# Where an adaLN gate vector is computed, and in which order a Strassen-like stage splits its operands

## The chip, the cores and the metric

One core of one Trainium2 chip runs the whole program. The metric is the device time of one execution in microseconds, as the median of several executions; lower is better.

## The reference, cut to what matters

Two streams, a prompt of 1024 tokens and a sample of 64, go through two layers with the same weights. Each layer has a mixing part (layer 0: attention and a linear recurrence side by side; layer 1: a gated recurrence) and a SwiGLU feed-forward part. Both are conditioned on a vector `c` per stream:

```
sc = silu(c)
m = (sc @ w_ada[l] + b_ada[l]).reshape(B, 6, 1024)
sh1, sc1, g1, sh2, sc2, g2 = m
hn = rms_norm(x, norm_mix[l]) * (1 + sc1) + sh1
x = x + (1 + g1) * mix(hn)
hn = rms_norm(x, norm_ffn[l]) * (1 + sc2) + sh2
x = x + (1 + g2) * ((silu(hn @ wg[l]) * (hn @ wu[l])) @ wd[l])
```

The model width is 1024 (8 tiles of 128 rows, `KD`), the hidden width of the feed-forward part 2816 (22 blocks of 128, `FF`). The gate `g2` of layer 0, group 5 of `m`, is what the change moves: 1024 values for each of the two streams.

## The kernel before, in words

Everything is held transposed: features on the 128 partitions, the 1088 tokens of both streams in the free dimension. fp32 matrices are split into a high part (rounded to fp32r, a cast on ScalarE) and a low part (source minus high, on GpSimd or VectorE), and each product is done as three matmuls: high by high, low by high, high by low.

Instructions are put in order for each engine ahead of the run by a list scheduler that simulates the program. A block under `soon()` (line 76) is preferred by it, a block under `later()` (line 79) is put off. The engine names with an `o` (`oV`, `oS`, `oPE`, lines 43 to 61) keep their instructions in the order in which the program writes them, on each engine among themselves; plain `V`, `S` and `PE` leave the order to the scheduler.

**Attention stage of layer 0** (lines 624 to 1167). The loop over four steps of two heads (lines 1126 to 1155) interleaves the score products and their sigmoids (`attn_w`, lines 877 to 880), the transposes and value products (`attn_o`) and the steps of the recurrence (`hgrn`). The input projections of the steps to come are put off, as filler; each takes its weights through `load_in` (line 1080), which uses a raw tile of two buffers (`raw_tile`, line 102). `load_in` also carries the conditioning: first two tiles of 128 rows of groups 2 to 4 a call, as dot products on VectorE (`mods_dve`), then, when these are done, one tile of group 5 a call: a load of 512 KB of `ada5`, 8 matmuls of two columns into a PSUM bank (line 1096), and a copy (line 1097).

**Feed-forward stage.** `enter` and `first_block` compute block 0 of the hidden layer the plain way. `up_half` (line 425) does block 1 the plain way (`plain_block`, in four chunks of tokens) and blocks 2 to 21 with a Strassen-like scheme: **seven products** of half size instead of eight, on sums of quarters of the input and sums of quarters of the weights. `sums` (line 467) makes the input's side: it adds the shift to the 8 tiles of `x` on ScalarE, forms four differences for each of four pairs of tiles (k and k + 4), and splits three of them into T3, T1 and T4 and then the last into T2. The products use their operands in the order B11, T2, T3, T1, B21, T4, B22 (line 488). T2 lies in tiles that block 1 has been reading. `weights` (line 450) makes the weights' side for each block: the first of its seven operands is a plain quarter, the second and third need the three additions of lines 455 to 457, all in program order on VectorE. Seven weights in high and low parts go through five buffers each. The accumulators X, Y, Z and W are read between the products by short instructions (`n1` to `p3`, lines 534 to 565).

**Conditioning in the feed-forward stage** (`Ada`, line 399). `open` loads the two conditioning vectors, spread over the partitions, and takes SiLU of them as sigmoid and multiply (`load_cbc`, line 183). Then each block has the slots `n1`, `n5` and, where the block number is under 8, `n2`. A slot does one tile: it takes a raw tile that was loaded ahead into one of two buffers and forms two dot products. In `n1` both are multiply-and-sum instructions on VectorE; in `n5` and `n2` (shared) the second is a multiply on GpSimd and a sum on ScalarE (lines 193 and 194). Their by-product goes to one scratch tile, `T[6]`. After eight tiles `finish_mods` adds the bias. In layer 0's stage 40 tiles (layer 1's groups 0 to 4) are done so, in layer 1's stage 8 (group 5). The second SiLU of a block (line 551) marks `n2`.

Of the kernel before, what the change touches and what calls it, by code (L numbers as in the profile page):

```python
# [54 lines left out]
def hybrid_encoder(ctx: ExitStack, tc: tile.TileContext, I, O):  # L55
# [114 lines left out]
    def finish_mods(l, i, j0=0, j1=KD):  # L170
        m = mods[l][:, i * KD + j0:i * KD + j1, :]
        b = vec[:, V_BADA + l * 48 + i * KD + j0:V_BADA + l * 48 + i * KD + j1]
        V.tensor_add(m, m, b.unsqueeze(2).to_broadcast([P, j1 - j0, 2]))
        if i in (2, 5):
            V.tensor_scalar_add(m, m, 1.0)
        if i in (1, 4):
            w = i // 3
            g = vec[:, V_NORM + (2 * l + w) * KD + j0:V_NORM + (2 * l + w) * KD + j1]
            V.scalar_tensor_tensor(scale[l][w][:, j0:j1, :], m, 1.0, g.unsqueeze(2).to_broadcast([P, j1 - j0, 2]),
                                   ALU.add, ALU.mult)  # L180


    def load_cbc(ts, sg):
        for v in range(2):
            dma(ts[v], I["cT2"][v:v + 1, :].partition_broadcast(P))
            S.activation(sg, ts[v], AF.Sigmoid)
            V.tensor_mul(ts[v], ts[v], sg)
        return ts

    def mods_dve(l, t, cb, raw, junk, shared=False, V=V):  # L190
        for v in range(2):
            if v and shared:
                G.tensor_mul(raw, raw, cb[v])
                S.activation(junk(), raw, AF.Identity, accum_out=mods[l][:, t, v:v + 1])  # L194
            else:
                V.scalar_tensor_tensor(junk(), raw, 1.0, cb[v], ALU.mult, ALU.mult,
                                       accum_out=mods[l][:, t, v:v + 1])
# [201 lines left out]
    class Ada:  # L399


        def __init__(self, todo):
            self.todo = [(i, j) for i in todo for j in range(KD)]

        def open(self, pool, raw, junk):
            self.raw, self.junk = raw, junk
            self.cb = load_cbc([pool.tile([P, 1024], F32, name="cbc", tag="cbc", bufs=2) for v in range(2)],
                               raw())
            self.ready = []

        def fetch(self, n):
            for _ in range(min(n, len(self.todo))):
                i, j = self.todo.pop(0)
                raw = self.raw()
                dma(raw, I["adaT"][48 + i * KD + j])
                self.ready.append((i, j, raw))

        def one(self, shared):
            if self.ready:
                i, j, raw = self.ready.pop(0)  # L420
                mods_dve(1, i * KD + j, self.cb, raw, self.junk, shared, oV)
                if j == KD - 1:
                    finish_mods(1, i)

    def up_half(l, plain, x, t_tag, op_tag, ada):
        B = B12, B11, B21, B22 = plain[0]
        with phase_pool(f"up{l}") as fp:
# [38 lines left out]

            def sums():

                for k in range(KD):
                    for r0, rn, b in rng(0, NT):  # L470
                        v = x[k][:, r0:r0 + rn]
                        oS.activation(v, v, AF.Identity, bias=mods[l][:, 3 * KD + k, b:b + 1])
                T1, T3, T4 = ([halves(fp.tile([P, NT], F32R, name="op", tag=t, bufs=4)) for _ in range(4)]
                              for t in ("t1", "t3", "t4"))
                for k in range(4):
                    a, b, c, d = x[k][:, :HT], x[k][:, HT:], x[k + 4][:, :HT], x[k + 4][:, HT:]
                    V.tensor_sub(d, b, d)
                    V.tensor_sub(b, b, a)
                    V.tensor_sub(a, a, d)
                    V.tensor_sub(c, c, a)  # L480
                    split(d, T3[k][:, 0, :], T3[k][:, 1, :], V, S=oS)
                    split(b, T1[k][:, 0, :], T1[k][:, 1, :], V, S=oS)
                    split(c, T4[k][:, 0, :], T4[k][:, 1, :], V, S=oS)
                T2 = []
                for k in range(4):
                    T2.append(halves(u(op_tag, F32R, "op")))
                    split(x[k][:, :HT], T2[k][:, 0, :], T2[k][:, 1, :], V)
                return B11, T2, T3, T1, B21, T4, B22

            stage["open"].close()  # L490
            with psum_pool(f"acc{l}", *(("acc" + n, 1024, 1) for n in "XYZW")):
# [31 lines left out]
                for f in range(2, FF):  # L523
                    if f == FF - 3:
                        assert not ada.todo and not ada.ready
                        got = [hid_units(i, t_tag) for i in range(GROUPS[0])]
                    X, Y, Z, W = (new_acc(n) for n in "XYZW")
                    x_, y_, z_, w_ = (t[:, :, :Q] for t in (X, Y, Z, W))
                    i = 2 * (f % 3) if f < FF - 3 else 4 + 2 * (f % 2)
                    tg, hid = T[i], T[i + 1]  # L530
                    pair = lambda t: t.rearrange("p (j t) -> p j t", j=2)
                    t, g, hA, hB = (pair(v) for v in (tg[:, :HT], tg[:, HT:], hid[:, :HT], hid[:, HT:]))

                    def n1():
                        S.copy(t, x_)
                        ada.one(False)
                        ada.fetch(1)

                    def n6():
                        oV.tensor_sub(t, y_, t)  # L540

                    def p7():
                        oV.tensor_add(hB, z_, t)

                    def n5():
                        oV.tensor_add(hB, w_, hB)
                        ada.one(True)
                        ada.fetch(1)

                    def n2():  # L550
                        S.activation(g, x_, AF.Silu)
                        if f < 8:
                            ada.one(True)
                            ada.fetch(1)

                    def p4():
                        oV.tensor_add(hA, z_, t)
                        oV.tensor_mul(hA, hA, g)
                        dma(hid_dram[f][:, :HT], hid[:, :HT])

                    def p3():
                        oV.tensor_add(t, w_, t)
                        S.activation(t, t, AF.Silu, scale=-1.0)
                        oV.tensor_mul(hB, hB, t)
                        dma(hid_dram[f][:, HT:], hid[:, HT:])

                    for acc, op, start, use in zip((X, Y, Z, W, X, Z, W), ops, (1, 1, 1, 1, 0, 0, 0),
                                                   (n1, n6, p7, n5, n2, p4, p3)):
                        w = ahead.pop(0)
                        for j in range(2):  # L570
                            product(acc, w, op, j, start)
                        for w in itertools.islice(queue, 1):
                            ahead.append(w)
                        with soon():
                            use()
# [48 lines left out]
    with phase_pool("mix") as mp:  # L624
# [450 lines left out]
                yield  # L1075

        todo = [(i, j) for i in (2, 3, 4) for j in range(KD)]
        todo_pe = list(range(KD))

        def load_in(t):  # L1080
            w = load_w(wi[t])
            with later():
                for _ in range(min(2, len(todo))):
                    i, j = todo.pop(0)
                    raw = raw_tile()
                    dma(raw, I["adaT"][i * KD + j])
                    mods_dve(0, i * KD + j, cb, raw, lambda: mp.tile([P, 1024], BF16, name="junk", tag="junk"))
                    if j == KD - 1:
                        finish_mods(0, i)
                if not todo and todo_pe:  # L1090
                    j = todo_pe.pop(0)
                    raw = raw_tile()
                    dma(raw, I["ada5"][j])
                    ps = bank("o")
                    for e in range(KD):
                        PE.matmul(ps[:, :2], raw[:, e * P:(e + 1) * P], sc[:, e, :], start=(e == 0), stop=(e == KD - 1))
                    V.tensor_copy(mods[0][:, 5 * KD + j, :], ps[:, :2])
                    if j == KD - 1:
                        finish_mods(0, 5)
            return w  # L1100

        def out_group(g, after=None, chunks=CH):
# [88 lines left out]


    stage["open"] = banks_open
    got = up_half(0, plain, x, "B", "A", Ada(range(5)))

    xg_open = ExitStack()
    xg = xg_open.enter_context(phase_pool("xg"))
# [199 lines left out]


    xg_open.close()
    got = up_half(1, plain, x, "A", "B", Ada((5,)))  # L1400
    with phase_pool("ffn1") as fp:
        stage["w"] = fp
        layout(fp, ("hid", 2 * NT, 2), ("late", 2 * NT, 1), ("wd_lo", 1024, 6), ("w_raw", 1024, 2),
# [123 lines left out]
def _layout(i):  # L1527
# [9 lines left out]
    d["cT2"] = t(c)  # L1537
    blk = lambda w: t(w.reshape(KD, P, -1, P).transpose(2, 1, 0, 3).reshape(-1, P, KD * P))
    d["ada0"] = blk(g["w_ada"][0][:, 1024:2048])
    d["ada5"] = blk(g["w_ada"][0][:, 5120:6144])  # L1540
    aT = np.concatenate([g["w_ada"][0], g["w_ada"][1]], axis=1)
    d["adaT"] = t(aT.T.reshape(96, P, 1024))
    d["w_in_even"] = blk(g["w_in_even"][0])
# [55 lines left out]
```

## Time and profile before

| | |
|---|---|
| median of 3 runs | 2803.64 us (2800.59 to 2804.72) |
| the profiled execution, its own time | 2801.73 us |
| its span, first to last instruction | 2800.0 us |
| TensorE matmul busy | 2616.5 us (93%) |
| VectorE busy | 1855.6 us (66%) |
| GpSimd busy | 1180.6 us (42%) |
| ScalarE busy | 1022.0 us (36%) |
| mean granted TensorE clock | 0.963 |

In the rows PE is TensorE's matmuls, PEld its weight loads, DVE VectorE, ACT ScalarE, POOL GpSimd and SP the queue that issues most loads. PEclk is the granted share of full clock: 1.00 is 2.4 GHz, 0.50 is 1.2 GHz. An instruction's record can overlap the one after it, so busy times are unions. Line 51 stands for every instruction that is kept in program order. A matmul of fp32 operands leaves two records.

### The profile page before, as it was taken

How to read it: one execution, taken by the hardware profiler on the slowest of the kernel's cores; microseconds unless marked ns; L12 is line 12 of the kernel's file. 1: busy time of each engine (PE TensorE's matmuls, PEld its weight loads, DVE VectorE, ACT ScalarE, POOL GpSimd, SP SyncE). 2: the span in 40 equal slices, each digit the busy share in tenths (PEclk: the TensorE clock that was granted, in tenths of full speed). 3: DMA queues.
4: the chain of work that ended last, by engine and by line, in shares of the span. 5: the costliest groups of instructions: out<-in, count | busy, mean ns of one | idle time of the engine just before them, and what ended most of it. 6: DMA issues, size and time to landing. Idle time of an engine off the chain costs nothing. (4 is left out here: it accounts for less than half of the span.)

```text
span 2800.0 us, 44597 instructions
## 1 busy us (share of the span) xinstructions
PE 2616.5 (93%) x17680; PEld 2553.8 (91%) x17680; DVE 1855.6 (66%) x2850; ACT 1022.0 (36%) x1862; POOL 1180.6 (42%) x795
## 2 busy tenths in 40 slices
PE   5898999999988899999999979998889999999998
PEld 5898989998878899999999979988889999999997
DVE  8768763667897778876465575658877444446556
ACT  3225343354454533333221146564363222222112
POOL 6446443455441477765322233444126444433112
PEclk8999989899999999999999989999999999999999
DMA  6232111113112344443432101121223222226211
GB/s 240 91 113 92 46 58 55 57 53 130 57 50 103 108 141 133 130 138 108 152 130 94 62 16 59 68 74 63 98 74 122 70 81 83 70 92 219 89 61 64
DMA packets 99663, 261.98 MB, mean 94 GB/s; under 512 B 16640, under 2 KB 36096, under 8 KB 99456
## 3 DMA queue, kind: packets, MB, share of 16 engines
q1 hardware_dynamic: 99168, 258.03, 27.7%
q8 instruction: 139, 2.28, 0.3%
q10 hardware_dynamic: 288, 1.11, 0.1%
q14 instruction: 68, 0.56, 0.1%
HBM read 208.41 MB, written 50.69 MB: 93 GB/s over the span
## 5 line engine op out<-in xcount | busy, mean ns | idle before, releaser
L100 POOL TENSOR_TENSOR w_lo<-w_raw,w_hi 128x1024 fp32r<-128x1024 f32 x92 | 237.3, 2586 | 533.9 <-ACT w_hi L99 484.6
L100 POOL TENSOR_TENSOR wl<-wg,wh 128x512 fp32r<-128x512 f32 x164 | 225.4, 1381 | 375.6 <-ACT wh L99 333.6
L507 PE MATMUL accZ<-op,wh 128*128 128x272 f32 x1280 | 245.5, 289 | 5.8 <-DVE tmp L51 5.7
L507 PE MATMUL accW<-op,wh 128*128 128x272 f32 x1280 | 244.3, 288 | 0.0
L507 PE MATMUL accX<-op,wh 128*128 128x272 f32 x1280 | 243.5, 288 | 0.0
L99 ACT CAST w_hi<-w_raw 128x1024 fp32r<-128x1024 f32 x90 | 93.2, 1050 | 362.3 <-PE ps_mm L313 253.5
L129 PE MATMUL ps_mm<-h_hi,w_hi 128*128 128x384 f32 (+1 forms) x624 | 213.2, 342 | 2.8 <-ACT w_hi L99 1.3
L129 PE MATMUL ps_mm<-h_hi,w_lo 128*128 128x384 f32 (+1 forms) x624 | 212.4, 342 | 2.0 <-POOL w_lo L100 2.0
L129 PE MATMUL ps_mm<-h_lo,w_hi 128*128 128x384 f32 (+1 forms) x624 | 212.0, 340 | 0.0
L507 PEld LDWEIGHTS accZ<-op,wh 128*128 128x128 f32 x1280 | 201.1, 188 | 7.6 <-DVE tmp L51 6.2
L99 ACT CAST wh<-wg 128x512 fp32r<-128x512 f32 x160 | 97.5, 619 | 296.9 <-DVE wg L51 191.4
L318 DVE SCALAR_TENSOR_TENSOR x<-ps_mm,mods,x 128x384 f32<-128x384 f32 (+4 forms) x334 | 152.2, 480 | 75.1 <-PE ps_mm L313 73.9
L507 PEld LDWEIGHTS accW<-op,wh 128*128 128x128 f32 x1280 | 201.3, 188 | 0.0
L507 PEld LDWEIGHTS accX<-op,wh 128*128 128x128 f32 x1280 | 200.9, 188 | 0.0
L507 PE MATMUL accZ<-op,wl 128*128 128x272 f32 x640 | 184.6, 288 | 1.0 <-POOL wl L100 1.0
L507 PE MATMUL accX<-op,wl 128*128 128x272 f32 x640 | 184.5, 288 | 0.0
L507 PE MATMUL accW<-op,wl 128*128 128x272 f32 x640 | 184.5, 288 | 0.0
L318 DVE SCALAR_TENSOR_TENSOR x<-ps_t,mods,x 128x384 f32<-128x384 f32 (+3 forms) x220 | 107.1, 504 | 87.9 <-PE ps_t L313 87.9
L51 DVE SCALAR_TENSOR_TENSOR tmp<-hid,cbc 128x1024 f32<-128x1024 f32 x68 | 132.0, 1941 | 21.6 <-ACT tmp L194 20.9
L100 POOL TENSOR_TENSOR wl<-wu,wh 128x512 fp32r<-128x512 f32 x84 | 131.7, 1569 | 27.9 <-ACT wh L99 27.3
L507 PE MATMUL accY<-op,wh 128*128 128x272 f32 x640 | 124.7, 292 | 16.1 <-ACT wh L99 16.1
L318 DVE SCALAR_TENSOR_TENSOR x<-ps_z,mods,x 128x384 f32<-128x384 f32 (+2 forms) x198 | 91.3, 485 | 61.4 <-PE ps_z L313 60.6
(485 smaller groups left out, 8066.1 us busy)
## 6 DMA issues: line engine op xcount, KB each, us to landing
hid<-in_adaT SPq DMA_DIRECT2D x48, 512.0 KB, 3.9
w_raw<-in_wd SPq DMA_DIRECT2D x44, 512.0 KB, 3.8
hid_dram<-tmp SPq DMA_DIRECT2D x80, 272.0 KB, 2.1
hid_lo<-hid_dram SPq DMA_DIRECT2D x40, 544.0 KB, 4.7
wg<-in_wg SPq DMA_DIRECT2D x42, 512.0 KB, 3.9
wu<-in_wu SPq DMA_DIRECT2D x42, 512.0 KB, 3.6
w_raw<-in_w_in_even SPq DMA_DIRECT2D x28, 512.0 KB, 3.7
w_raw<-in_adaT SPq DMA_DIRECT2D x24, 512.0 KB, 3.6
```

The costliest lines, as they stand in the source:

```text
L51: return lambda *a, **k: self.tc.keep_in_program_order(f(*a, **k))
L99: S.copy(hi, src)
L100: (lo_eng or G).tensor_sub(lo, src, hi.bitcast(F32))
L129: PE.matmul(ps[:, :n], a[:, k * P:(k + 1) * P], b[:, c0:c0 + n], start=(i == 0), stop=(i == last))
L318: V.scalar_tensor_tensor(x[m][:, r0:r0 + rn], ps[:, r0 - c0:r0 - c0 + rn], gate[:, m, b:b + 1], x[m][:, r0:r0 + rn], ALU.mult, ALU.add)
L507: PE.matmul(acc[:, j, :Q], a[:, k * P:(k + 1) * P], op[k][:, b, c], start=(start == 1 and i == 0), stop=(i == 11), skip_group_check=True)
```

## The change

Four edits. The gate of layer 0 (group 5) leaves `load_in` and becomes the first eight tiles of the `Ada` of layer 0's seven-product stage, which so has 48. The number of blocks with a third slot is now worked out from the number of tiles: below block `thrice`, which is 16 with 48 tiles and 2 with the 8 tiles of layer 1's stage. The SiLU of the conditioning vectors is one ScalarE instruction in place. In `sums` the shift goes over the tiles in pairs, the differences come first, then the splits for T2, T3, T1 and T4 in this order, and all of it is kept in program order on VectorE and ScalarE.

```
-    def load_cbc(ts, sg):
+    def load_cbc(ts):
         for v in range(2):
             dma(ts[v], I["cT2"][v:v + 1, :].partition_broadcast(P))
-            S.activation(sg, ts[v], AF.Sigmoid)
-            V.tensor_mul(ts[v], ts[v], sg)
+            S.activation(ts[v], ts[v], AF.Silu)
...
-            self.todo = [(i, j) for i in todo for j in range(KD)]
+            self.todo = [(l, i, j) for l, i in todo for j in range(KD)]
+            self.thrice = 2 + max(0, len(self.todo) - 2 * (FF - 5))
...
-                dma(raw, I["adaT"][48 + i * KD + j])
+                dma(raw, I["adaT"][48 * l + i * KD + j])
...
-                for k in range(KD):
+                for k in (0, 4, 1, 5, 2, 6, 3, 7):
                     for r0, rn, b in rng(0, NT):
                         v = x[k][:, r0:r0 + rn]
                         oS.activation(v, v, AF.Identity, bias=mods[l][:, 3 * KD + k, b:b + 1])
...
+                T2 = []
+                part = lambda k: (x[k][:, :HT], x[k][:, HT:], x[k + 4][:, :HT], x[k + 4][:, HT:])
                 for k in range(4):
-                    a, b, c, d = x[k][:, :HT], x[k][:, HT:], x[k + 4][:, :HT], x[k + 4][:, HT:]
-                    V.tensor_sub(d, b, d)
-                    V.tensor_sub(b, b, a)
-                    V.tensor_sub(a, a, d)
-                    V.tensor_sub(c, c, a)
-                    split(d, T3[k][:, 0, :], T3[k][:, 1, :], V, S=oS)
-                    split(b, T1[k][:, 0, :], T1[k][:, 1, :], V, S=oS)
-                    split(c, T4[k][:, 0, :], T4[k][:, 1, :], V, S=oS)
-                T2 = []
+                    a, b, c, d = part(k)
+                    oV.tensor_sub(d, b, d)
+                    oV.tensor_sub(b, b, a)
+                    oV.tensor_sub(a, a, d)
                 for k in range(4):
                     T2.append(halves(u(op_tag, F32R, "op")))
-                    split(x[k][:, :HT], T2[k][:, 0, :], T2[k][:, 1, :], V)
+                    split(part(k)[0], T2[k][:, 0, :], T2[k][:, 1, :], oV, S=oS)
+                for k in range(4):
+                    split(part(k)[3], T3[k][:, 0, :], T3[k][:, 1, :], oV, S=oS)
+                for k in range(4):
+                    split(part(k)[1], T1[k][:, 0, :], T1[k][:, 1, :], oV, S=oS)
+                for k in range(4):
+                    a, b, c, d = part(k)
+                    oV.tensor_sub(c, c, a)
+                    split(c, T4[k][:, 0, :], T4[k][:, 1, :], oV, S=oS)
...
-                        if f < 8:
+                        if f < ada.thrice:
                             ada.one(True)
                             ada.fetch(1)
...
-                if not todo and todo_pe:
-                    j = todo_pe.pop(0)
-                    raw = raw_tile()
-                    dma(raw, I["ada5"][j])
-                    ps = bank("o")
-                    for e in range(KD):
-                        PE.matmul(ps[:, :2], raw[:, e * P:(e + 1) * P], sc[:, e, :], start=(e == 0), stop=(e == KD - 1))
-                    V.tensor_copy(mods[0][:, 5 * KD + j, :], ps[:, :2])
-                    if j == KD - 1:
-                        finish_mods(0, 5)
...
-    got = up_half(0, plain, x, "B", "A", Ada(range(5)))
+    got = up_half(0, plain, x, "B", "A", Ada([(0, 5)] + [(1, i) for i in range(5)]))
...
-    got = up_half(1, plain, x, "A", "B", Ada((5,)))
+    got = up_half(1, plain, x, "A", "B", Ada([(1, 5)]))
```

## Rows read from the trace of the kernel before

**Rows 1.** Busy time by stretch: stretch, length, PE, PEld, DVE, ACT, POOL, PEclk, DMA share, GB/s

```profile
340.00:560.00 220.00, 211.01 (x1322) 201.18 (x1321) 122.59 (x191) 81.99 (x187) 90.52 (x72) 0.88 0.18 56
...
750.00:800.00 50.00, 42.85 (x266) 37.07 (x265) 49.96 (x84) 32.08 (x77) 33.34 (x32) 1.00 0.21 60
946.00:1372.00 426.00, 419.37 (x3316) 417.36 (x3316) 315.02 (x336) 138.23 (x242) 276.05 (x162) 1.00 0.38 121
```

**Rows 2.** Waits of ScalarE, 340 to 560 us: us in total, times, longest

```profile
ACT om L879 <- PE ps_z L877: 22.9, 17, 3.9
```

**Rows 3.** Line 1096: its busy time, then timeline rows (start, length) of TensorE

```profile
340.00:560.00 220.00, 20.03 (x128) 21.04 (x128) 0.88 0.18 56
...
434.71 2.96 PE L1096 MATMUL ps_o<-sc,w_raw 128*128 128x2 f32 x26
437.53 1.18 PE L912 MATMUL ps_o<-wt,vs 128*128 128x256 f32 x8
...
395.63 3.51 PE L1096 MATMUL ps_o<-sc,w_raw 128*128 128x2 f32 x16
```

**Rows 4.** Busy time by stretch, short stretches of the attention stage

```profile
488.00:492.00 4.00, 4.00 (x34) 3.89 (x33) 3.72 (x8) 0.48 (x1) 3.78 (x4) 0.91 0.39 137
492.00:508.00 16.00, 15.62 (x61) 14.45 (x62) 9.00 (x12) 5.66 (x10) 7.54 (x5) 0.50 0.39 125
...
395.00:409.00 14.00, 14.00 (x59) 13.44 (x59) 9.25 (x11) 7.42 (x17) 9.33 (x7) 0.50 0.31 97
```

**Rows 5.** Timeline of ScalarE, line 551: blocks 4 to 10, then layer 1's 4 and 5

```profile
1001.11 0.62 ACT L551 ACTIVATE tmp<-accX 128x544 f32<-128x544 f32 x1 [1.05 <-PE accX L507]
...
1024.86 0.62 ACT L551 ACTIVATE tmp<-accX 128x544 f32<-128x544 f32 x1 [1.18 <-PE accX L507]
...
1046.28 0.62 ACT L551 ACTIVATE tmp<-accX 128x544 f32<-128x544 f32 x1
...
1069.34 0.62 ACT L551 ACTIVATE tmp<-accX 128x544 f32<-128x544 f32 x1
...
1091.99 0.61 ACT L551 ACTIVATE tmp<-accX 128x544 f32<-128x544 f32 x1
...
1113.74 0.63 ACT L551 ACTIVATE tmp<-accX 128x544 f32<-128x544 f32 x1 [2.37 <-PE accX L507]
...
1134.79 0.62 ACT L551 ACTIVATE tmp<-accX 128x544 f32<-128x544 f32 x1 [4.12 <-PE accX L507]
...
2148.02 0.62 ACT L551 ACTIVATE tmp<-accX 128x544 f32<-128x544 f32 x1 [1.10 <-PE accX L507]
...
2170.86 0.62 ACT L551 ACTIVATE tmp<-accX 128x544 f32<-128x544 f32 x1 [4.66 <-PE accX L507]
```

**Rows 6.** Timeline of VectorE and GpSimd in layer 0's seven-product stage

```profile
957.96 2.78 POOL L193 TENSOR_TENSOR hid<-hid,cbc 128x1024 f32<-128x1024 f32 x1 [1.90 <-DVE tmp L51]
...
958.57 2.72 DVE L51 TENSOR_TENSOR wu<-wg,wu 128x512 f32<-128x512 f32 x1
...
1006.99 0.18 DVE L173 TENSOR_TENSOR mods<-mods,vec 128x16 f32<-128x16 f32 x1 [3.74 <-ACT tmp L194]
...
1033.34 2.11 DVE L51 SCALAR_TENSOR_TENSOR tmp<-hid,cbc 128x1024 f32<-128x1024 f32 x1 [2.26 <-ACT tmp L194]
```

**Rows 7.** Timeline, start of layer 0's stage, and TensorE's longest wait there

```profile
910.30 8.83 ACT L51 ACTIVATE x<-x,mods 128x1024 f32<-128x1024 f32 x13
...
916.83 0.72 DVE L477 TENSOR_TENSOR x<-x 128x544 f32<-128x544 f32 x1 [9.09 <-ACT x L51]
...
926.68 1.22 DVE L187 TENSOR_TENSOR cbc<-cbc,hid 128x1024 f32<-128x1024 f32 x1
...
929.09 2.62 DVE L100 TENSOR_TENSOR op<-x,op 128x544 fp32r<-128x544 f32 x4
...
943.28 0.68 DVE L51 TENSOR_TENSOR wg<-s,wg 128x512 f32<-128x512 f32 x1
...
PE accY L507 <- ACT wh L99: 7.9, 1, 7.9
```

More of the change, by code (lines that the diff above doesn't have):

```diff
@@ L402, in __init__ @@
         def __init__(self, todo):
-            self.todo = [(i, j) for i in todo for j in range(KD)]
+            self.todo = [(l, i, j) for l, i in todo for j in range(KD)]
+            self.thrice = 2 + max(0, len(self.todo) - 2 * (FF - 5))
         def open(self, pool, raw, junk):
             self.raw, self.junk = raw, junk
-            self.cb = load_cbc([pool.tile([P, 1024], F32, name="cbc", tag="cbc", bufs=2) for v in range(2)],
-                               raw())
+            self.cb = load_cbc([pool.tile([P, 1024], F32, name="cbc", tag="cbc", bufs=2) for v in range(2)])
             self.ready = []
@@ L412, in fetch @@
             for _ in range(min(n, len(self.todo))):
-                i, j = self.todo.pop(0)
+                l, i, j = self.todo.pop(0)
                 raw = self.raw()
-                dma(raw, I["adaT"][48 + i * KD + j])
-                self.ready.append((i, j, raw))
+                dma(raw, I["adaT"][48 * l + i * KD + j])
+                self.ready.append((l, i, j, raw))
         def one(self, shared):
             if self.ready:
-                i, j, raw = self.ready.pop(0)
-                mods_dve(1, i * KD + j, self.cb, raw, self.junk, shared, oV)
+                l, i, j, raw = self.ready.pop(0)
+                mods_dve(l, i * KD + j, self.cb, raw, self.junk, shared, oV)
                 if j == KD - 1:
-                    finish_mods(1, i)
+                    finish_mods(l, i)
     def up_half(l, plain, x, t_tag, op_tag, ada):
@@ L1077, in hybrid_encoder @@
         todo = [(i, j) for i in (2, 3, 4) for j in range(KD)]
-        todo_pe = list(range(KD))
         def load_in(t):
@@ L1539, in _layout @@
     d["ada0"] = blk(g["w_ada"][0][:, 1024:2048])
-    d["ada5"] = blk(g["w_ada"][0][:, 5120:6144])
     aT = np.concatenate([g["w_ada"][0], g["w_ada"][1]], axis=1)
```

## The prediction

> **What bounds the kernel now.** I read the page first: TensorE is busy for 93% of the span and every other engine for two thirds or less, so a change counts where it takes TensorE work away or makes TensorE wait. The view of busy time by stretch shows this for the three places that the change touches [rows 1]. In the attention stretch from 340 to 560 us TensorE is busy 211.0 of 220 us and VectorE 122.6. At 750 to 800 VectorE is the full one, with 49.96 of 50. In the first seven-product stage, 946 to 1372, TensorE is busy 419.4 of 426, VectorE 315, GpSimd 276. The waits of ScalarE in the attention stretch then say who is late there: the sigmoids of the scores waited 22.9 us in 17 places for a score product on TensorE [rows 2]. The attention chain itself stands behind TensorE's queue, so TensorE time taken out of this stretch should come off the end.
>
> **Part 1: 64 products per condition pair leave attention.** The eight tiles of the gate are 8 x 8 matmuls of two columns. The trace has 128 records for them (two for each), busy 20.03 us [rows 3]. Their busy time overlaps the next group: the run of 26 at 434.71 lasts to 437.67, while the next matmul starts at 437.53, 0.14 us before. Some fifteen such groups make about 2 us of overlap, so I take **-18 us**. Bounds: all 128 at the pace of the run at full clock (26 in 2.96 us) 14.6 us, all at the pace of the slow run (16 in 3.51 us) 28.1 us; nothing at all if the stretch is not bound by TensorE (a rival). With them go eight 512 KB loads on SP's queue, eight small copies on VectorE, and the use of the two-buffer raw tile and of a PSUM bank between weight loads; none of these engines is full in the stretch [rows 1], so I price them at nothing, and a gain from earlier weights lies within the upper bound.
>
> **Part 2: the same tiles come back as dot products.** In the first seven-product stage 48 tiles instead of 40 are conditioned. Two per block of the hidden layer as before; a third one, so far in blocks 2 to 7, now in blocks 2 to 15. Each third is a VectorE multiply-and-sum, a GpSimd multiply of 2.78 us and a ScalarE sum, and a load. DMA engines are busy 38% there [rows 1] and take the load for nothing. The rest is not free. The start of the second SiLU marks each block [rows 5]: from block 9 to 10, with two per block, it recurs after 21.05 us, which is TensorE's own pace. From block 5 on, with three, after 21.42, 23.06 and 22.65, a mean excess of 1.33 us, with 0.70 left over in block 8. The mechanism is in rows 6: at 1033.34 the third's VectorE instruction waited 2.26 us for the ScalarE sum of the tile before it (both write the same scratch tile), and behind it in VectorE's order stand the additions that free the accumulators which TensorE needs next. Eight more such blocks cost 8 x 1.33 = 10.6 us. When a group of eight ends on a shared tile, the closing addition waits for ScalarE too (3.74 us at 1006.99), and block 4, where that happened, took 23.75, an excess of 2.70; the second half's only stretched block, 22.84, is the same case. Groups now end so in blocks 9 and 12: 2 x 1.4 more. Sum **+13.4 us**, bounds 8 x 0.37 = 3 and 8 x 2.70 = 21.6. The end values are single blocks; a mean of three is nearer to what eight will do. The gate's own values are first read after this stage, so nobody waits for them.
>
> One row also prices the shared multiply from the other side: beside the GpSimd multiply that began at 957.96 a VectorE addition took 2.72 us, while 0.72 or less is usual for this size [rows 6, 7]. The Trainium skill, SBUF — State Buffer, section Who interferes with whom, speaks against this part of the change: VectorE with two SBUF inputs and a reading GpSimd take one shared port in turns, and the loser waits for the whole instruction. The trace agrees with it (2.72 for the addition). By that alone each further multiply would put some 2.0 us on VectorE, an estimate of 16.2 us for eight in place of 13.4.
>
> **Part 3: the second half.** Its eight tiles are now spread two per block. The stretched block of 22.84 us [rows 5] should fall to the pace: **-1.8 us** (0 to -1.8).
>
> **Part 4: the start of both seven-product stages.** Today TensorE waits 7.9 us before the second product [rows 7]; the record names the cast of the weights, which stands behind a sum on VectorE that starts at 943.28, itself in a stretch of VectorE without a gap from 916.83. The change makes four edits there. (a) ScalarE shifts tiles 0, 4, 1, 5 ... in that order. Thirteen pieces take 8.83 us, so about 1.3 us for a tile; the first pair is complete after two tiles and not five, and VectorE starts 3.9 us earlier. But then pairs come each 2.6 us and three subtractions need 1.9, so the last pair's end lies at about 923.2. (b) The two 1.22 us multiplies of the conditioning vector go (Silu at once), about 2.3 us of VectorE. (c) The halves are cut in the order in which products use them: T2 no longer comes last. (d) All of it stands in program order, and so **ahead of the weight sums**, which today are put between. After 923.2 come sixteen cuts and four subtractions at 0.65 us [rows 7], 13.1 us, four multiplies of the plain block's hidden rows, some 1.6 us, and in the last group each cut must wait for the cast of what was subtracted just before it, about 0.65 us four times, half of it covered by those multiplies: 939.3 to 940.6. Then three weight sums of 0.6 to 0.7: 941.2 to 942.6, against 943.9 today. I take **-1.7 us for each stage, -3.4** together. Bounds: 0, and -7.9 each if T2 alone had been late. Silu also spares table changes on ScalarE, which is not what is late there.
>
> **Sum.** -18 + 13.4 - 1.8 - 3.4 = **-9.8 us**. The profiled execution took 2801.73 us (span 2800.0 and 1.7 around it), so 2791.9 for its like; the median of the runs is 1.9 above it, so the forecast is **2793.8 us**. A measurement of this kernel tells about 0.2%, 5.6 us, from no change: faster means under 2798.0, slower over 2809.2.
>
> **Rivals.**
> *The clock comes back too.* At 395 to 409 and at 492 to 508 the granted clock was 0.50, the 1.2 GHz level, and before the second of these TensorE was busy 4.00 of 4 us, mostly with the two-column products [rows 4]. Of these 30 us let a third be the products themselves; the other 20 us would take half at 2.4 GHz, 10 us less: 2783.8. Against it: bursts of other narrow products stand close by and may hold the clock down without these. The Trainium skill, TensorE: Matmul & The Clock Gate, Part 1, ties the lower level to idleness; by that rule removing busy matmuls gives no clock back, and the row with 4.00 of 4 does not agree with it. Chance 0.25.
> *The freed time is not on the path.* Slower: at 750 to 800 VectorE is full [rows 1], and if attention ends when VectorE's chain there ends, whatever TensorE did before, part 1 is worth nothing and the rest makes +13.4 - 5.2 = +8.2: 2811.8. It decides if VectorE's work up to there does not move ahead with TensorE's. Against it: rows 2, and VectorE's idle 97 us in the stretch. Chance 0.12.
> *The thirds pile up.* If blocks 8 to 15 each lose 2.70 us, the sum is -18 + 21.6 - 5.2 = -1.6: 2802.0, no difference that can be told. Chance 0.15.
> *T2 was the gate.* If the order of the cuts does what its form suggests, each start gives 7.9 us: -22.2, 2781.4. Against it is the late weight sum. Chance 0.08.
>
> **How the numbers follow.** The forecast case has 0.40. Its own range, with part 1 from 15 to 21 us and the thirds from 10 to 16, is 2788 to 2800. Faster takes most of it (0.36) with the clock's 0.25 and T2's 0.08, together 0.69; the same takes 0.04 and the pile-up's 0.15, 0.19; slower the uncovered path, 0.12. The range reaches from 2775, where the clock comes back and the dot products are cheaper than 1.33, to 2808, leaving the slower rival mostly out.
>
> **What would show it.** Part 1 right: no two-column products between 340 and 560, the seven-product stage starts some 18 us earlier (its first plain matmul is at about 909 today). Part 2: SiLU spacing of 22 to 23 us in blocks 4 to 15 and not only to 8. Part 3: no stretched block in the second half. Part 4: a wait before the second product of about 6 us, still for a weight. The forecast is wrong if the stage's start moves by under 10 us, if blocks 8 to 15 keep 21.05, or if attention's granted clock rises well above 0.88.

## The result, and the profile after

The changed kernel takes **2771.4 us** (median of 4 runs, 2768.4 to 2778.4) where the kernel before takes 2802.8: a ratio of 0.9897, with a 95% interval of 0.9875 to 0.9919. Run again beside other kernels it gave 0.9913 (0.9898 to 0.9928). The forecast of 2793.8 had the sign right and a third of the size, and its range began at 2775.

To see where the time went I cut the span at two marks that every version has: the first matmul of block 1's plain product in each feed-forward stage, and the second SiLU of block 21, the last. The stretches of the profiled execution, before and after, in us: up to the first mark 908.9 and 863.6 (**-45.3**); from there to block 21's SiLU 459.4 and 474.8 (**+15.4**); on to the second stage's mark 687.6 and 689.3 (+1.7); the second stage to its block 21 452.1 and 447.0 (**-5.1**); the rest 292.0 and 293.2 (+1.2). The sum is -32.1, the difference of the spans, 2800.0 and 2767.9.

**Attention.** Busy time of the changed kernel in the attention stage's middle (stretch, length, PE, PEld, DVE, ACT, POOL, PEclk, DMA share, GB/s), and the same view of the kernel before:

```profile
280.00:600.00 320.00, 310.67 (x2090) 296.47 (x2089) 214.90 (x309) 142.96 (x332) 159.37 (x129) 0.99 0.16 47
```

```profile
280.00:600.00 320.00, 309.14 (x1958) 295.18 (x1956) 188.69 (x283) 121.41 (x277) 134.36 (x109) 0.91 0.17 54
```

TensorE is as busy as it was, 97% of the stretch, so the busy column shows nothing. The clock does: 0.91 against 0.99. At two levels of 1.00 and 0.50, a mean of 0.91 over 320 us is 57.6 us at half speed, and 0.99 is 6.4 (0.98, or 12.8, in the second profile of the same kernel). In the same 320 us VectorE did 215 us of work and not 189. This is what answers to the first row of [rows 1] and to [rows 4].

**The start of the seven products.** TensorE's wait for a weight between 850 and 960 us (total, times, longest) and VectorE's timeline there, answering to [rows 7]:

```profile
PE accY L511 <- ACT wh L99: 1.9, 1, 1.9
```

```profile
889.27 0.68 DVE L51 TENSOR_TENSOR s<-wu 128x512 f32<-128x512 f32 x1
...
891.93 0.69 DVE L51 TENSOR_TENSOR wg<-s,wg 128x512 f32<-128x512 f32 x1
...
903.62 0.72 DVE L51 TENSOR_TENSOR op<-x,op 128x544 fp32r<-128x544 f32 x1 [0.71 <-ACT op L51]
```

The wait before the second product fell from 7.9 to 1.9 us. The weight sums (s at 889.27, wg at 891.93) stand ahead of the last split of T4 (903.62), not behind it.

**The thirds.** The second SiLU of blocks 8 to 13, answering to [rows 5]; a block's time is counted from its own SiLU to the next block's:

```profile
1043.47 0.61 ACT L555 ACTIVATE tmp<-accX 128x544 f32<-128x544 f32 x1
...
1066.14 0.61 ACT L555 ACTIVATE tmp<-accX 128x544 f32<-128x544 f32 x1
...
1094.71 0.63 ACT L555 ACTIVATE tmp<-accX 128x544 f32<-128x544 f32 x1 [3.25 <-PE accX L511]
...
1136.81 0.63 ACT L555 ACTIVATE tmp<-accX 128x544 f32<-128x544 f32 x1
...
1162.04 0.63 ACT L555 ACTIVATE tmp<-accX 128x544 f32<-128x544 f32 x1 [1.38 <-PE accX L511]
```

With three tiles block 8 takes 22.67 us (1043.47 to 1066.14), as such a block did before. Block 9, whose third tile ends a group, takes 28.57; blocks 10 and 11 are at TensorE's pace, 42.10 for both; block 12, where a group ends on a shared tile too, takes 25.23. What happens in block 9, on VectorE, on TensorE (in brackets the wait), and in the view by stretch:

```profile
1082.64 0.18 DVE L173 TENSOR_TENSOR mods<-mods,vec 128x16 f32<-128x16 f32 x1 [4.65 <-ACT tmp L193]
```

```profile
1083.81 0.56 PE L511 MATMUL accZ<-op,wh 128*128 128x272 f32 x2 [5.00 <-DVE tmp L51]
```

```profile
1085.00:1090.00 5.00, 5.00 (x33) 5.00 (x32) 4.24 (x8) 0.66 (x1) 0.00 (x0) 0.75 0.73 246
```

VectorE stands 4.65 us for ScalarE's sum, TensorE 5.00 behind it, and then the clock is granted at 0.75 of full over the next 5 us: 33 matmuls where the 5 us windows around it at 1.00 hold 41 to 43.

### The profile page after: what moved, and what is told of

Read it like the earlier page. It is cut to its first block, busy times and chain, and to the rows that moved or that the text cites. A ratio compares the mean times of both kernels' runs of the same rounds, so it can differ in the third digit from the quotient of the medians.

```text
span 2767.9 us, 44376 instructions
## 1 busy us (share of the span) xinstructions
PE 2588.9 (94%) x17552; PEld 2525.6 (91%) x17552; DVE 1883.2 (68%) x2856; ACT 1016.1 (37%) x1868; POOL 1204.6 (44%) x802
## 4 chain that ended last, share of the span: by engine, by line
PE 41%; DVE 8%; ACT 3%; issue 1%; DMA 0%; POOL 0%; DVEq 0%; SPq 0%; ACTq 0%; POOLq 0%
PE ps_t L312 7%; PE ps_mm L312 7%; PE ps_z L312 7%; PE accZ L511 5%; PE accW L511 5%; PE accX L511 5%; PE accY L511 2%; DVE xc L51 2%; DVE mu L51 1%; DVE rg L51 1%; PE ps_t L51 1%; ACT rg L51 1%; PE ps_z L51 1%; DVE x L317 1%; ACT mu L51 1%
## 5 line engine op out<-in xcount | busy, mean ns | idle before, releaser
L511 PE MATMUL accZ<-op,wh 128*128 128x272 f32 x1280 | 249.2, 292 | 18.8 <-DVE tmp L51 18.8
L51 DVE SCALAR_TENSOR_TENSOR tmp<-hid,cbc 128x1024 f32<-128x1024 f32 x77 | 150.9, 1960 | 36.0 <-ACT tmp L193 35.3
```

The source lines that it names most:

```text
L51: return lambda *a, **k: self.tc.keep_in_program_order(f(*a, **k))
L511: PE.matmul(acc[:, j, :Q], a[:, k * P:(k + 1) * P], op[k][:, b, c], start=(start == 1 and i == 0), stop=(i == 11), skip_group_check=True)
```

## The experiments

The theory: attention's gain is the two-column products' own time and, as much again, the clock that they cost; the thirds cost what VectorE waits for on the shared path over GpSimd and ScalarE. Rivals: the loads and the raw tile's turns held attention back; the stage start carries the gain; the thirds cost VectorE's own work. The kernel before moved between chips by up to 9 us in its median, so ratios are to the kernel before on the same chip, and the terms are read from the stretches:

| kernel | ratio to before, 95% | first mark | SiLU of block 2 after it | of block 21 | second stage, block 21 |
|---|---|---|---|---|---|
| before | 1 | 908.9 | 50.1 | 459.4 | 452.1 |
| after | 0.9897 (0.9875 to 0.9919) | 863.6 | 43.0 | 474.8 | 447.0 |
| after_again | 0.9913 (0.9898 to 0.9928) | 866.5 | 45.9 | 474.5 | 446.6 |
| e1_move_only | 0.9935 (0.9920 to 0.9950) | 870.3 | 50.0 | 478.0 | 450.5 |
| e2_start_only | 0.9968 (0.9951 to 0.9985) | 903.9 | 45.9 | 455.8 | 448.6 |
| e3_narrow | 1.0017 (1.0008 to 1.0026) | 909.1 | 43.4 | 471.9 | 446.2 |
| e4_wide | 0.9967 (0.9953 to 0.9981) | 886.8 | 43.4 | 472.0 | 444.4 |
| e5_forty | 0.9839 (0.9818 to 0.9860) | 872.5 | 43.0 | 456.0 | 445.3 |
| e6_scratch | 0.9863 (0.9842 to 0.9884) | 871.5 | 43.0 | 464.5 | 444.4 |
| e7_late | 0.9887 (0.9864 to 0.9910) | 867.4 | 46.0 | 469.8 | 443.9 |
| e8_both | 0.9883 (0.9860 to 0.9905) | 872.1 | 45.9 | 464.0 | 446.9 |
| e9_t2last | 0.9922 (0.9903 to 0.9942) | 869.7 | 46.3 | 473.2 | 448.6 |
| e10_sigmoid | 0.9925 (0.9906 to 0.9944) | 870.3 | 46.2 | 475.0 | 448.4 |
| e11_order | 0.9908 (0.9886 to 0.9930) | 864.7 | 45.8 | 474.9 | 446.2 |
| e12_load | 0.9924 (0.9900 to 0.9948) | 867.3 | 44.5 | 473.8 | 446.0 |
| e13_own_end | 0.9853 (0.9838 to 0.9867) | 868.4 | 45.8 | 457.2 | 446.6 |
| e14_thirds_dve | **0.9809** (0.9793 to 0.9826) | 869.8 | 45.8 | 445.9 | 443.7 |

**Taking the change apart: e1_move_only and e2_start_only.** The first is the changed kernel with `sums` and `load_cbc` of the kernel before; the second is the kernel before with those of the changed one.

> The changed kernel with the old start of the seven-product stages (old order of shifts, differences and splits, sigmoid and multiply for the conditioning vectors). Stage by stage the changed trace reads: attention -45 us, start of each seven-product stage -7, blocks of the first +22.5, blocks of the second -1. If these are separate effects, this kernel is 13 to 15 us slower than the changed one, about 2785, the wait before the second product is back at 8 us in both stages, and the attention stage ends as early as in the changed one. If the attention gain hangs on the new start (one common list of instructions, scheduled together), the first plain matmul of block 1 is later than 870 us.

> The kernel before with the new start of the two seven-product stages alone; the gate's conditioning stays in attention. Separate effects: about 2803 - 14 = 2789 us, first plain matmul of block 1 at 909 us as before, waits before the second product near 2 us, blocks of the first stage as before (excess of 7.4 us over blocks 2 to 8). If the weight sums stood strictly behind all splits, as the prediction had it, the wait would be about 6 us and the gain under 4 us.

The effects are separate. Where the products have left attention the first mark lies between 863.6 and 872.5 in twelve profiles (mean 868.9); with them in, at 908.9, 903.9 and 909.1 (mean 907.3): **-38 us**, and the 863.6 of the first profile was a low one. The new start alone is worth 459.4 - 455.8 = 3.6 and 452.1 - 448.6 = 3.5 us, about **-7** for both and not the 14 that I read at block 2: TensorE's wait of e1 is back at 8.0 and of e2 down at 1.9, but in the first stage the blocks with three tiles are not ready sooner and take a part back (in e2 block 2 is 4.2 us earlier, block 21 3.6), and in the second stage the clock can still fall after the short wait: 45.9 us to block 2 in eight versions whose start there is written alike, 43.4 in five others.

**The products' time or their clock: e3_narrow, e4_wide, e12_load.** The first puts line 1096's loads and products back beside the change. The others alter that block:

```
-                    for e in range(KD):
-                        PE.matmul(ps[:, :2], raw[:, e * P:(e + 1) * P], sc[:, e, :], start=(e == 0), stop=(e == KD - 1))
+                    for e in range(2 * KD):
+                        PE.matmul(ps[:, :272], w[0][:, (e % KD) * P:(e % KD + 1) * P], h[0][e % KD][:, :272],
+                                  start=(e == 0), stop=(e == 2 * KD - 1))
```

for e4_wide, and no matmul at all, the load alone, for e12_load (the load stays in e4_wide too).

> The changed kernel, with the two-column products of the gate done in attention as well (their results are copied to a spare tile that nobody reads). If it is these products and what hangs on them that cost the 45 us, the attention stage is back at about 909 us for the first plain matmul of block 1, the whole near 2771 + 45 = 2816 us, and the granted clock between 350 and 550 us falls from 1.00 to below 0.9. If only their own TensorE time counted, 18 to 20 us: about 2790.

> As the kernel with the narrow products in attention, but in their place 16 matmuls of 272 columns on operands that are there anyway (the projection's weights and input, result not read) for each of the eight tiles, 128 in all at about 0.125 us, 16 us of TensorE; the eight 512 KB loads into the same raw tile stay. If the clock is the larger part of the loss, it stays at 1.00 here and the stage ends 16 to 20 us later than in the changed kernel, about 2789 us. If the loads and the raw tile's turn-taking are the cause, it is as slow as the narrow one, about 2812 to 2816.

> The changed kernel with the eight 512 KB loads in attention as before, read by a small copy only, without any matmul. If the loads and their turn in the raw tile hold back the projections' weights, part of the 45 us returns (10 us or more); if they were free, as the prediction had it, the attention stage ends within 3 us of the changed kernel's.

The first mark comes at 909.1, 886.8 and 867.3. The loads cost nothing that the mark shows. Against the mean of 868.9, 128 wide matmuls of 0.125 us, 16 us of TensorE, cost 18; 128 records of narrow ones, busy 20.03 us [rows 3], cost 40. Each mark is that of one execution, and the one profiled of e3_narrow was the slowest of its ten (2810.6 us, median 2806.3): by the medians of the two on one chip, narrow costs 16.1 us more than wide, not 22.3. The view by stretch of e3_narrow, e4_wide and e12_load:

```profile
280.00:600.00 320.00, 310.40 (x1967) 296.25 (x1966) 189.77 (x281) 121.24 (x276) 135.19 (x110) 0.91 0.18 55
```

```profile
280.00:600.00 320.00, 309.27 (x2059) 294.48 (x2059) 209.85 (x305) 133.96 (x305) 148.78 (x121) 0.97 0.18 58
```

```profile
280.00:600.00 320.00, 312.10 (x2070) 298.62 (x2070) 214.30 (x315) 141.52 (x328) 155.28 (x129) 0.97 0.20 62
```

As many matmul records come from the same point of the program. With 272 columns the clock is 0.97, as it is with no products at all in e12_load; with 2 columns it is 0.91. So about half of attention's gain is the clock for everybody else. Which property of the narrow products takes the clock is not shown: the wide ones differ in their operands as well (fp32r instead of fp32, weights that are used anyway). The whole of e3_narrow is 10 us under the 2816 that I expected: I had added 45 us where 38 is the usual size.

**The price of the thirds: e5_forty.** `Ada([(0, 5)] + [(1, i) for i in range(4)])`.

> The changed kernel with 40 tiles of conditioning in the first seven-product stage instead of 48: the last group, layer 1's feed-forward scale, is left out and set to constants, so its conditioning is missing from the output. Thirds stop after block 7 again. If the eight thirds cost what the block spacing says, this stage is 19 to 23 us shorter and the whole about 2750 us; by the prediction's price it would be 13 us, 2758.

The first stage is 474.8 - 456.0 = **18.8 us** shorter (18.5 against the second profile), just under the first expectation's 19 and well over the 13.4 of the prediction. The whole, 2757.4 us, is near the 2758 of the second expectation, but it was measured on another chip: by the ratios to the kernel before (0.9839 against 0.9897 and 0.9913) the eight tiles cost 16 to 21 us.

**What the thirds wait for: e6_scratch, e7_late, e8_both.** A second scratch tile `T[7]` for `mods_dve`'s ScalarE sum; `finish_mods` called two slots later; both.

> The changed kernel with a second scratch tile: the by-product of the ScalarE sum goes to T[7], that of VectorE's stays in T[6]. If the thirds cost their 22 us because VectorE's next multiply-and-sum waits for ScalarE to write the same scratch tile (25 waits, 35 us on VectorE in the changed trace), the blocks with three tiles come down to 21.05 to 21.5 us except where a group ends, and the whole falls by 8 to 14 us. If VectorE's own work or the port that it shares with GpSimd sets the 22.7 us of such a block, the spacing stays and so does the time.

> The changed kernel with the closing addition of a group done two slots later. If the blocks where a group ends on a shared tile (28.57 and 25.23 us, and 25.11 in block 4) are long because VectorE stands still for ScalarE's sum in that addition (four waits, 15.8 us), they come down to the 22.7 of their neighbours, 8 to 11 us in all. If the addition is only where a longer chain shows, nothing changes.

> The changed kernel with both: a second scratch tile and the closing addition two slots later. If the two waits are the whole price of the thirds, all blocks come near 21.05 us and the whole is 18 to 22 us faster than the changed kernel, about 2750 us. If there is a third limit behind them (the raw tile's two buffers, GpSimd's queue), some blocks stay at 22 us or more and the gain stays under 15.

The stage comes from 474.8 to 464.5, 469.8 and 464.0. The scratch tile is worth 10 us, later closing 5, both together no more than the first (in the whole less: 2770.0 us against e6_scratch's 2762.7): later in the program is not later in the queue, and in e8_both the closing addition still stood for ScalarE, in block 9, which took 28.95. TensorE's longest wait in total in e6_scratch, 915 to 1345:

```profile
PE accZ L511 <- POOL wl L100: 7.6, 11, 1.0
```

With the scratch wait gone the next in line shows: GpSimd is late with the low parts of weights.

**The rest of it: e13_own_end and e14_thirds_dve.** On top of e6_scratch:

```
-                mods_dve(l, i * KD + j, self.cb, raw, self.junk, shared, oV, self.junk2)
+                mods_dve(l, i * KD + j, self.cb, raw, self.junk, shared and j < KD - 1, oV, self.junk2)
```

and for e14_thirds_dve `ada.one(False)` in `n2` too.

> The changed kernel with the second scratch tile, and the last tile of each group of eight done on VectorE alone, so that the closing addition waits for no ScalarE sum. With the second scratch tile alone block 9 still takes 27.58 us and block 12 22.48. If the closing addition's wait for ScalarE is what stretches block 9, it comes down to 22 us or less, the stage by 5 to 7 us more, the whole to about 2756 us. If GpSimd's splits, which are the more frequent wait now (11 waits, 7.6 us), are the limit, block 9 falls but its neighbours stay at 22.

> As the kernel before it in this list, with both dot products of each third tile on VectorE and none on GpSimd. If the remaining excess of about 0.9 us in a block with three tiles comes from GpSimd (2.8 us for the multiply between the weight splits), these blocks come to 21.05 us; if VectorE's own work is then too long, they grow to 23 us or more.

> The changed kernel itself, beside the two others on the same chip: 2768 to 2775 us; the attention stage ends between 863 and 873 us, since other versions with the same attention stage spread over that much.

A group's last tile on VectorE alone takes block 9's stretch away (22.28 us) and leaves most blocks with three tiles near 22. TensorE's main wait in e13_own_end's first stage, then GpSimd and TensorE in block 8:

```profile
PE accZ L511 <- POOL wl L100: 6.6, 10, 0.8
```

```profile
1053.34 2.88 POOL L192 TENSOR_TENSOR hid<-hid,cbc 128x1024 f32<-128x1024 f32 x1
1056.17 1.28 POOL L100 TENSOR_TENSOR wl<-wu,wh 128x512 fp32r<-128x512 f32 x1
...
1057.50 0.39 PE L511 MATMUL accZ<-op,wl 128*128 128x272 f32 x1 [0.57 <-POOL wl L100]
```

The third's multiply stands in GpSimd's queue ahead of a weight's split, and TensorE waits for that split.

Thirds on VectorE alone bring every block to pace. SiLU rows of e14_thirds_dve, blocks 8 and 9, an addition of VectorE there, and its stretch of the stage:

```profile
1041.91 0.62 ACT L555 ACTIVATE tmp<-accX 128x544 f32<-128x544 f32 x1 [3.01 <-PE accX L511]
...
1062.96 0.62 ACT L555 ACTIVATE tmp<-accX 128x544 f32<-128x544 f32 x1 [3.21 <-PE accX L511]
```

```profile
1042.80 2.71 DVE L51 TENSOR_TENSOR wu<-wg,wu 128x512 f32<-128x512 f32 x1
```

```profile
915.00:1336.00 421.00, 416.41 (x3284) 415.92 (x3283) 347.68 (x388) 127.80 (x223) 248.57 (x149) 0.99 0.44 143
```

VectorE now does 348 us in 421, and TensorE waits for it nowhere in this stretch: its own work was not the limit. Nor was the addition: it takes 2.71 us here too, beside a multiply on GpSimd that began at 1042.18, and the block is at pace. The stage takes 445.9 us, 13.5 less than in the kernel before and 10.1 less than in e5_forty, with eight tiles more than either. At 2745.4 us (2798.6 before on that chip) this is the **best version**, faster than both kernels.

**Which edit shortens the start: e9_t2last, e10_sigmoid, e11_order.** T2's split written last; sigmoid and multiply; tiles in the order 0 to 7.

> The changed kernel with the split for T2 written last again; shift order, program order and Silu stay. If T2's place is what shortens the wait before the second product from 8 to 2 us, the wait is back at 8 us or more in both stages and the kernel 12 us or more slower, about 2784. If the weights are the gate, as the record names them, nothing changes: 2771.

> The changed kernel with sigmoid and multiply for the conditioning vectors, as before: two VectorE multiplies of 1.2 us and four changes of ScalarE's table of 1.28 us come back at the start of each seven-product stage. If they are on the path to the second product, the wait grows by 2 to 5 us in each stage and the whole by 4 to 10; if they are put beside it, nothing changes.

> The changed kernel with the shift over the tiles in the order 0 to 7: VectorE's first difference starts 3.9 us later. If the start of VectorE's stretch counts to its end, the wait before the second product grows by 2 to 4 us in each stage, 4 to 8 in all; if VectorE waits for ScalarE anyway, by under 1.

TensorE's wait for a weight between 850 and 960 in the first two, in this order (in e11_order it is 1.9, as in the changed kernel):

```profile
PE accY L511 <- ACT wh L99: 4.0, 1, 4.0
```

```profile
PE accY L513 <- ACT wh L99: 3.6, 1, 3.6
```

T2 first takes 2.1 us off the wait and the single Silu 1.7; the order of the shift takes nothing (VectorE waits for ScalarE anyway). All undone it is 8.0 (e1_move_only), so 2.3 more belong to program order or to the edits acting together; I did not take these apart. My expectation of 8 us for T2 alone was a miss, and so was that of 2 to 4 for the order of the shift.

## Why the prediction was wrong, step by step

**Part 1, -18 us: measured -38 (-45 in the first profile). This is the step that failed.** The own time was right: 18 us for the wide stand-in of 16 us, 20.03 us busy for the narrow ones. The clock stood at nothing in the sum; it was put among the rivals as *the clock comes back too*, at a chance of 0.25 and 10 us. It was not a rival but a second term of the same part, and nearly twice as large, 16 us by the medians and 20 by the marks: I had counted 30 us at half speed in two stretches by eye, while the view of the whole stretch says 57.6, and it falls to 6.4 (19.2 in e12_load, which has the loads alone). The objection that other narrow products would hold the clock down was wrong. The one in the Trainium skill (TensorE: Matmul & The Clock Gate, Part 1), which ties the lower level to idleness, does not fit: with TensorE busy for 97% of the stretch both times, the clock fell in one and not in the other. That the loads cost nothing was right (e12_load), and so was that TensorE bounds the stretch: *the freed time is not on the path* is out.

**Part 2, +13.4 us: measured +18.6.** Blocks 8 to 15 of the changed kernel lie 17.0 us over the pace in sum. The six ordinary ones have 5.2 of it, where 6 x 1.33 = 8.0 was forecast: blocks 8, 14 and 15 lose 1.6 to 1.8, and 10, 11 and 13 next to nothing. Blocks 9 and 12 have 11.7, where 5.5 was forecast. Too small was the price of a group that ends on a shared tile: 1.4 us above the others in block 4 of the kernel before, but 2.6 in block 12 and 5.9 in block 9, where TensorE stood for 5.00 us and the clock fell right behind. The mechanism was a part of it. From the changed kernel's 474.8 us to the 445.9 of e14_thirds_dve are 28.9 us, 10.1 of which 40 tiles cost as well (e5_forty, 456.0): the scratch tile is 10.3 of them (to 464.5, e6_scratch), the closing addition 7.3 (to 457.2, e13_own_end), and 11.3 go when the multiply on GpSimd and the sum on ScalarE leave `n2`. TensorE's waits put 6.6 of these on the weight splits queued behind that multiply, which I had not named; the rest I cannot place. The rule of the Trainium skill on the shared port (SBUF — State Buffer, Who interferes with whom) gave 16.2, nearer than my sum, and the trace agrees with its direction, since moving the multiply from GpSimd to VectorE made each block faster. That it came nearer was luck: its price was time on VectorE, and e14_thirds_dve keeps an addition of 2.71 us beside a multiply and runs at TensorE's pace. What share the port has in the waits on VectorE is not shown.

**Part 3, -1.8 us:** right; the stretched block of 22.84 us is gone (21.05 in all later profiles with this change); two blocks near the end of the stage gave 0.7 of it back in the first profile.

**Part 4, -3.4 us: measured -7.** Step (d) was wrong. Instructions that are kept in program order do not stand strictly as written where some of them are preferred: the weight sums of `soon()` came out ahead of T4's splits. So the weights were ready sooner than I worked out, and T2's place and the single Silu both counted. What I took for a bound, 7.9 each, is nearly reached in the wait (6.0) and not in the time (3.5).

**The case that came true** is the clock's, with larger terms in parts 1, 2 and 4. The measured terms make -38 + 18.6 - 1.8 - 7 = -28 us, between the two results of -31 and -25. The range missed since the clock was kept as an alternative to the sum and not put into it.

## What to carry to other kernels

Read a stretch's granted clock beside its busy share before pricing the removal of small matmuls: their own time can be half of what they cost, and the busy column does not show the other half. Price a wait that stops TensorE for some microseconds with the slower matmuls behind it. Before sharing work among engines, ask which queue it joins: here the added work on VectorE was free, while the multiply on GpSimd, the sum on ScalarE and the waits that they bring cost 28.6 us in one stage (after_again 474.5, e14_thirds_dve 445.9).

## What the runs showed of the hardware

With two-column fp32 products among wide ones TensorE was busy for 97% of 320 us and its clock 0.91 of full in the mean, which is 57.6 us at 1.2 GHz. With 272-column fp32r matmuls in their place it was 0.97 (19.2 us), and with none 0.97 to 0.99 (19.2 to 6.4, in e12_load and the changed kernel). I had not expected 20 us of instructions to cost the matmuls around them so much.

After a short wait the clock is not the same from one execution to the next. In two profiles of the changed kernel the first stage has the same wait of 1.9 us; behind it stand these rows, of the first profile and of after_again:

```profile
895.00:900.00 5.00, 5.00 (x40) 5.00 (x41) 5.00 (x5) 1.00 (x2) 5.00 (x3) 1.00 0.02 5
```

```profile
900.00:905.00 5.00, 5.00 (x33) 5.00 (x33) 5.00 (x4) 0.65 (x1) 5.00 (x4) 0.76 0.07 8
```

The clock stayed at 1.00 in one and fell to 0.76 in the other, and block 2 came 43.0 and 45.9 us behind the mark.
